# Hymba-style decoder step: norm weights moved into the output projection's rows, block-diagonals of the exponents written by ScalarE

## The chip, the cores and the metric

One core of one Trainium2 chip. The metric is the device time of one launch in microseconds (us). TensorE (PE; PEld is its weight load), VectorE (DVE), ScalarE (ACT), GpSimd (POOL) and SyncE (SP, which only issues transfers) run their own instruction streams in order and wait for each other through semaphores.

## The reference

One layer of a hybrid decoder runs on a prompt of 16 + 1024 tokens and on 8 running sequences of 4 tokens. Width 1024; two mixers of width 512 side by side; an MLP of width 4096. All is float32.

```python
def rmsnorm(x, g):
    return x * lax.rsqrt(jnp.mean(x * x, -1, keepdims=True) + EPS) * g

u = rmsnorm(h, norm1_g) @ w_in            # q, k, v, z, xbc, dt
ao = sliding_window_attention(q, k, v)    # window 128, with sinks
so = rmsnorm(ssd_scan(conv(xbc), dt) * silu(z), ssm_out_g)
mix = concatenate([rmsnorm(ao, attn_out_g), so], -1)      # 512 + 512
h = h + mix @ w_out                       # w_out: 1024 x 1024
u = relu(rmsnorm(h, norm2_g) @ w_up)
h = h + (u * u) @ w_down
y = rmsnorm(h, norm_f_g)
```

Since `(x * g) @ W = x @ (g[:, None] * W)`, the weights `attn_out_g` and `ssm_out_g` can stand on the mixers' outputs or on the rows of `w_out`.

## The kernel before, in words

Activations lie transposed: features on the 128 partitions, tokens in the free dimension. Tokens are cut in tiles of 128 (a small first tile of 48 holds the running sequences and the meta tokens) and, for the projections, in three chunks of 384, 384 and 288 columns. Every float32 operand of a large product is split in a rounded part and a remainder (hi and lo), and three products are added; `gemm` does this (all its matmuls carry line 202).

The stages in time:

- 0 to about 300 us: input projection, convolution and, per tile, `attn_block` and `norm_o`.
- about 300 to 407 us: the SSD per tile (`ssd`, `gate`), between pieces of the first half of the output projection (`wout_stream`: attention rows of `w_out`, eight row blocks m by three chunks). `exponents` prepares two groups of four tiles, near 306 and near 352 us: L, Tr and R, block-diagonal operands of small matmuls.
- about 407 to 457 us: the second half (`mixer_half`: SSD rows of `w_out`), chunks 0 and 1 first, then chunk 2, for which the eight blocks are loaded a second time. Of each m, GpSimd issues a transfer `he<-ha`; the squares for the next norm are summed, and GpSimd takes its power (`rs`, line 321).
- 457 us to the end: the MLP.

`load_wout` is called 24 times, 16 for `m` and `half` and 8 for the second pass of chunk 2. It transfers a raw block of 128x512 (SP's queue), ScalarE casts it (hi, line 243), and GpSimd or VectorE takes the remainder (lo, line 244). The raw tiles, `wraw`, come from a ring of two buffers, hi and lo from two rings of two. `Ahead` calls it one to three blocks ahead of use.

`norm_o` and `gate` end with four VectorE instructions (j = 0..3) that multiply a 128x128 quarter of the tile by its column of `vec` (the norm weight) and by the reciprocal root, which stands in PSUM.

Before the first SSD tile, GpSimd loads `selr` (line 909) and copies the small tile's columns to `xs0` and `bc0` (lines 944 and 946; the trace names them xs and bc). TensorE transposes them at lines 1038 and 1040.

The order of each engine's instructions is not the order of the Python code alone. The build sets it with a list scheduler, which follows operands, buffers and its own costs, so an edit also moves instructions that it does not touch.

Of the kernel before, what the change touches and what calls it, by code (L numbers as in the profile page):

```python
# [11 lines left out]
AF = mybir.ActivationFunctionType  # L12
ALU = mybir.AluOpType
# [37 lines left out]
def _consts():  # L51
    p = np.arange(128)[:, None]
    f = np.arange(128)[None, :]
    cols = {}
    parts = []
    at = [0]

    def put(name, a):
        a = np.asarray(a, np.float32)
        full = np.zeros((128, a.shape[1]), np.float32)  # L60
        full[:a.shape[0]] = a
        cols[name] = (at[0], at[0] + a.shape[1])
        at[0] += a.shape[1]
        parts.append(full)

    put("ident", np.eye(128))
    put("tri", (p <= f))
    blk = np.zeros((48, 48))
    for b in range(8):
        blk[4 * b:4 * b + 4, 4 * b:4 * b + 4] = 1  # L70
    blk[32:, 32:] = 1
    put("tri0", blk * (np.arange(48)[:, None] <= np.arange(48)[None, :]))
    put("blk0", blk)
    delta = np.zeros((128, 8))
    mm = np.zeros((128, 2))
    sel = np.zeros((128, 4, 128))
    for r in range(128):
        k = r % 32
        delta[r, k % 8] = 1
        if k < 16:  # L80
            for j in range(4):
                for hh in range(2):
                    if k % 8 == 2 * j + hh:
                        sel[r, j, hh * 64:hh * 64 + 64] = 1
            mm[r] = (0, 1)
        else:
            mm[r] = (1, 0)
    put("delta", delta)
    put("mm", mm)
    put("seqm", np.tile(np.kron(np.eye(8), np.ones((4, 1))), (3, 1)))  # L90
    resident = at[0]
    put("sel", sel.reshape(128, 512))


    pos = np.zeros(T, np.float32)
    for t in range(T):
        pos[t] = 4096 + t % 4 if t < NSAMP else t - NSAMP
    inv = (500000.0 ** (-np.arange(8) / 8.0)).astype(np.float32)
    ang = (pos[None, :] * inv[:, None]).astype(np.float32).astype(np.float64)
    cos, sin = np.ones((128, T)), np.zeros((128, T))  # L100
    for g in range(2):
        for half in range(2):
            rows = slice(64 * g + 8 * half, 64 * g + 8 * half + 8)
            cos[rows], sin[rows] = np.cos(ang), np.sin(ang) * (1 if half else -1)
    put("cos", cos)
    put("sin", sin)
    attn = at[0]

    prev, cur = np.where(f > p, 0.0, NEG), np.where(f <= p, 0.0, NEG)
    put("mask", np.concatenate([prev, cur, prev], axis=1))  # L110
    m1 = np.full((128, 48), NEG)
    for m in range(16):
        m1[:112 + m, 32 + m] = 0.0
    put("mask1", np.concatenate([m1, cur], axis=1))
    ms = np.full((2, 128, 160), NEG)
    for s in range(2):
        for r in range(128):
            b, t = 4 * s + r // 32, r % 4
            ms[s, r, t + 1:128] = 0.0
            ms[s, r, 128 + 4 * b:128 + 4 * b + t + 1] = 0.0  # L120
    put("maskS", ms.transpose(1, 0, 2).reshape(128, 320))

    cols["resident"], cols["rope_"], cols["attn_"] = (0, resident), (attn - 2 * T, attn), (attn, at[0])
    return np.concatenate(parts, axis=1), cols
# [62 lines left out]
def f(ap):  # L187
    return ap.bitcast(F32)
# [3 lines left out]
def body(ctx: ExitStack, tc: tile.TileContext, xT, xm, win, wdt, wo, wu, wd, ck, cv, sc, st, sT, vec, consts,  # L192
# [44 lines left out]
    def load_wout(m, half, eng=POOL):  # L237

        raw = raw_tile()[:, 0:4, :]
        SP.dma_start(out=raw, in_=wo[m, half])  # L240
        tag = "wlo" if m % 2 else "whi"
        hl = wring.tile([128, 2, 4, 128], F32R, name=tag, tag=tag, bufs=2)
        ACT.copy(out=hl[:, 0], in_=raw)
        eng.tensor_tensor(out=hl[:, 1], in0=raw, in1=f(hl[:, 0]), op=ALU.subtract)
        return hl[:, 0], hl[:, 1]
# [508 lines left out]
    def norm_o(i, o_ps=None):  # L754
# [2 lines left out]
        sq = pa.tile([128, 4, 128], F32, name="sqo", tag="sqo", bufs=1)  # L757
        ACT.activation(out=sq[:, :, :rows], in_=o if o_ps is None else o_ps[:, :, :rows], func=AF.Square)
        ps = yield from rms_bcast(pa, POOL, ps_tile, sq[:, :, :rows], rows, 512, "o", "pt")
        for j in range(4):  # L760
            DVE.scalar_tensor_tensor(out=o[:, j], in0=o[:, j], scalar=vec[:, V_GA + j:V_GA + j + 1], in1=ps[:, :rows],
                                     op0=ALU.mult, op1=ALU.mult)

    def attn_sample():
        kcT, vc = caches
# [147 lines left out]
    def exponents(rows, w, s):  # L913
        n = w // 32
        tp = ptile()
        PE.transpose(tp[:w, :rows], A4[:rows, s, :], ident[:rows, :rows])
        if n > 1:
            L = sp.tile([128, 4, 128], F32R, name="L", tag="L", bufs=1)
            Tr = sp.tile([128, 4, 128], F32R, name="Tr", tag="Tr", bufs=1)
            R = sp.tile([128, 8, 128], F32R, name="R", tag="R", bufs=1)  # L920
            POOL.memset(f(L), 0.0)
            POOL.memset(f(Tr), 0.0)
        else:
            L = sp.tile([128, 1, T0], F32R, name="L0")
            Tr = sp.tile([128, 1, T0], F32R, name="Tr0")
# [3 lines left out]
        for h in range(0, 8, 4):  # L929
            DVE.tensor_tensor(out=R[:w, h:h + 4, :rows], in0=tm[:w, :rows].unsqueeze(1).broadcast_to([w, 4, rows]),  # L930
                              in1=c("delta", w)[:, h:h + 4].unsqueeze(2).broadcast_to([w, 4, rows]), op=ALU.mult)
        for q in range(n):
            rr = slice(32 * q, 32 * q + 32)
            DVE.tensor_scalar(out=L[rr, q, :rows], in0=tp[rr, :rows], scalar1=mmc[rr, 0:1], scalar2=mmc[rr, 1:2],
                              op0=ALU.mult, op1=ALU.add)
# [233 lines left out]
    def gate(i):  # L1169
# [7 lines left out]
        ACT.activation(out=sq[:, :, :rows], in_=y, func=AF.Square)  # L1177
        yield
        ps = yield from rms_bcast(sp, DVE, ptile, sq[:, :, :rows], rows, 512)
        for j in range(4):  # L1180
            DVE.scalar_tensor_tensor(out=y[:, j], in0=y[:, j], scalar=vec[:, V_GS + j:V_GS + j + 1], in1=ps[:, :rows],
                                     op0=ALU.mult, op1=ALU.mult)
        hi, lo = act_cols(X, i)
        ACT.copy(out=hi, in_=y)
        POOL.tensor_tensor(out=lo, in0=y, in1=f(hi), op=ALU.subtract)
# [645 lines left out]
```

## Time and profile before

| | |
|---|---|
| median of 3 runs | 1131.54 us (1131.04 to 1132.6) |
| profiled execution | 1130.17 us, of which the span is 1128.4 us |
| busy, share of the span | TensorE 98%, VectorE 75%, ScalarE 50%, GpSimd 20% |
| granted TensorE clock | 0.998 |
| loads of `w_out` blocks | 24 of 256 KB, median 3.0 us from issue to landing |

The times shown are those of one launch; the profile is one execution of it, whose time is slightly below the median. In the profile, a group of instructions shares line, engine, operation and tile; the chain of waits is followed back from the last instruction to what released each step.

### The profile page before, as it was taken

How to read it: one execution, taken by the hardware profiler on the slowest of the kernel's cores; microseconds unless marked ns; L12 is line 12 of the kernel's file. 1: busy time of each engine (PE TensorE's matmuls, PEld its weight loads, DVE VectorE, ACT ScalarE, POOL GpSimd, SP SyncE). 2: the span in 40 equal slices, each digit the busy share in tenths (PEclk: the TensorE clock that was granted, in tenths of full speed). 3: DMA queues.
4: the chain of work that ended last, by engine and by line, in shares of the span. 5: the costliest groups of instructions: out<-in, count | busy, mean ns of one | idle time of the engine just before them, and what ended most of it. 6: DMA issues, size and time to landing. Idle time of an engine off the chain costs nothing.

```text
span 1128.4 us, 21816 instructions
## 1 busy us (share of the span) xinstructions
PE 1110.6 (98%) x8405; PEld 1071.9 (95%) x8405; DVE 841.9 (75%) x1649; ACT 567.6 (50%) x1200; POOL 225.0 (20%) x292
## 2 busy tenths in 40 slices
PE   9999999999999999999999999999999999999997
PEld 8989988989888899999999999999999999999996
DVE  6646888985698968998877777766599656768483
ACT  8312456575575748854444444444434334546461
POOL 0442365654444441210000000000000000000010
PEclk9999999999999999999999999999999999999999
DMA  8131101111476476666652443425999653465273
GB/s 289 68 98 38 38 23 35 39 49 46 136 217 194 147 260 227 212 186 220 211 189 106 162 152 134 176 92 176 374 310 322 197 173 103 125 196 166 77 228 107
DMA packets 84424, 177.64 MB, mean 157 GB/s; under 512 B 10692, under 2 KB 32740, under 8 KB 82272
## 3 DMA queue, kind: packets, MB, share of 16 engines
q1 hardware_dynamic: 77392, 141.58, 40.1%
q0 software_dynamic: 6224, 33.74, 7.5%
q8 instruction: 66, 1.08, 0.4%
q10 hardware_dynamic: 704, 0.93, 0.2%
q14 instruction: 38, 0.31, 0.1%
HBM read 125.49 MB, written 50.72 MB: 156 GB/s over the span
## 4 chain that ended last, share of the span: by engine, by line
PE 81%; DVE 7%; ACT 6%; issue 2%; DMA 2%; POOL 1%; SPq 0%; POOLq 0%; DVEq 0%; ACTq 0%
PE g L202 43%; PE b L202 21%; PE c L202 10%; PE s L202 3%; ACT p L677 1%; PE o L202 1%; DVE Qs L708 1%; DMA wraw<-in_win 1%; PE y L202 1%; PE pt L741 1%; DVE p L675 1%; ACT whi L231 1%; PE pt L202 0%; DVE xs L524 0%; ACT acth L407 0%
## 5 line engine op out<-in xcount | busy, mean ns | idle before, releaser
L202 PE MATMUL g<-acth,whi 128*128 128x384 f32 (+2 forms) x528 | 161.7, 330 | 0.2 <-DVE qT L454 0.2
L202 PE MATMUL g<-acth,wlo 128*128 128x384 f32 (+2 forms) x528 | 159.3, 327 | 0.2 <-DVE hb L985 0.2
L202 PE MATMUL g<-actl,whi 128*128 128x384 f32 (+2 forms) x432 | 140.7, 326 | 0.0
L1613 ACT CAST ts<-tr 128x528 fp32r<-128x528 f32 x92 | 58.2, 632 | 116.3 <-PE b L202 97.3
L1614 DVE TENSOR_TENSOR ts<-tr,ts 128x528 fp32r<-128x528 f32 x92 | 65.1, 707 | 54.9 <-ACT ts L1613 54.2
L202 PEld LDWEIGHTS g<-acth,whi 128*128 128x128 f32 x528 | 97.3, 188 | 2.0 <-issue 1.0
L202 PEld LDWEIGHTS g<-acth,wlo 128*128 128x128 f32 x528 | 97.1, 188 | 0.6 <-DVE hb L985 0.4
L202 PEld LDWEIGHTS g<-actl,whi 128*128 128x128 f32 x432 | 81.4, 188 | 0.2
L321 POOL TENSOR_TENSOR rs<-rs,nhalf 128x3 f32<-128x3 f32 x9 | 10.6, 1179 | 333.2 <-DMA wdq<-in_wd 284.9
L1329 ACT COPY s<-g 128x264 f32<-128x264 f32 x90 | 33.8, 376 | 61.7 <-PE g L202 61.1
L234 POOL TENSOR_TENSOR wlo<-wraw,whi 128x256 fp32r<-128x256 f32 x56 | 49.9, 921 | 11.4 <-ACT whi L231 11.3
L1402 POOL DMA_DIRECT2D u<-u x16 | 8.5, 532 | 176.3 <-ACT u L1345 146.9
L1334 DVE TENSOR_TENSOR u<-b,s 128x264 f32<-128x264 f32 x64 | 27.5, 430 | 19.2 <-PE b L202 9.8
L731 POOL TENSOR_TENSOR p<-p,sm 128x512 f32<-128x512 f32 (+1 forms) x32 | 34.9, 1112 | 30.2 <-DVE sm L729 28.4
L1339 ACT ACTIVATE u<-u 128x528 f32<-128x528 f32 x42 | 27.2, 647 | 26.6 <-DVE u L1338 26.6
L202 PE MATMUL b<-ts,w7y 128*128 128x264 f32 x279 | 39.3, 285 | 0.0
L202 PE MATMUL g<-ts,whi 128*128 128x264 f32 x279 | 38.9, 284 | 0.0
L202 PE MATMUL g<-ts,w7y 128*128 128x264 f32 x279 | 38.9, 283 | 0.0
L202 PE MATMUL b<-ts,whi 128*128 128x264 f32 x279 | 38.9, 284 | 0.0
L202 PE MATMUL g<-ts,wlo 128*128 128x264 f32 x270 | 38.0, 285 | 0.0
L202 PE MATMUL b<-ts,wlo 128*128 128x264 f32 x270 | 37.3, 282 | 0.0
L677 ACT ACTIVATE p<-p,nm 128x257 f32<-128x257 f32 (+1 forms) x64 | 31.3, 492 | 10.1 <-DVE nm L675 10.0
(580 smaller groups left out, 3479.1 us busy)
## 6 DMA issues: line engine op xcount, KB each, us to landing
tr<-u SPq DMA_DIRECT2D x92, 264.0 KB, 3.0
wraw<-in_wu SPq DMA_DIRECT2D x38, 512.0 KB, 4.1
wdr<-in_wd SPq DMA_DIRECT2D x68, 256.0 KB, 3.8
u<-t POOLq DMA_DIRECT2D x16, 1056.0 KB, 5.5
wraw<-in_win SPq DMA_DIRECT2D x16, 512.0 KB, 3.7
u<-u POOLq DMA_DIRECT2D x10, 792.0 KB, 3.6
wraw<-in_wo SPq DMA_DIRECT2D x24, 256.0 KB, 3.0
h<-he SPq DMA_DIRECT2D x16, 264.0 KB, 4.7
```

Of the source, the lines that this page charges most:

```text
L202: PE.matmul(out, lhsT=a, rhs=b, start=start, stop=stop, skip_group_check=on)
L231: ACT.copy(out=hi[:, k], in_=raw[:, k])
L234: eng.tensor_tensor(out=lo[:, n], in0=raw[:, n], in1=f(hi[:, n]), op=ALU.subtract)
L675: DVE.tensor_tensor_reduce(out=s_out[:, 0:W], in0=ps, in1=mask, scale=-scale, scalar=nsink, op0=ALU.add, op1=ALU.min, accum_out=nm)
L677: ACT.activation(out=s_out[:, 0:W + 1], in_=s_out[:, 0:W + 1], func=AF.Exp, bias=nm, scale=-1.0, accum_out=sm)
L708: DVE.tensor_tensor(out=Q[oth, g, :, :rows], in0=src, in1=f(Q[own, g, :, :rows]), op=ALU.subtract)
L731: POOL.tensor_tensor(out=p[:rows, r:r + 2, :W], in0=p[:rows, r:r + 2, :W], in1=sm[:rows, r:r + 2].unsqueeze(2).broadcast_to([rows, 2, W]), ...
L1329: ACT.copy(out=s[:, c], in_=ps[c][:, :TQ])
L1334: DVE.tensor_tensor(out=out[:, c], in0=ps[c][:, :TQ], in1=s[:, c], op=ALU.add)
L1339: ACT.activation(out=x, in_=x, func=AF.Square)
L1613: ACT.copy(out=t[:, 0], in_=x)
L1614: DVE.tensor_tensor(out=t[:, 1], in0=x, in1=f(t[:, 0]), op=ALU.subtract)
```

## The change

The norm weights no longer act on the mixers' outputs. `load_wout` multiplies each raw block's four row groups by the weights on GpSimd, in place, between the transfer and the cast (4 x 128 columns, the weight read with stride 0). The four instructions at the end of `norm_o` and of `gate` become one `tensor_tensor` of 128x512. In `exponents`, the groups of four write each of the four blocks of L and Tr whole, 128 partitions with zeros from a mask in the constants (`ownL`, `own`), by ScalarE; the memsets of GpSimd, the four VectorE instructions for L and the four narrow copies for Tr are gone. The small tile keeps its form.

```diff
+    own = np.arange(128)[:, None] // 32 == np.arange(4)[None, :]
+    put("ownL", np.concatenate([own * mm[:, 0:1], own * mm[:, 1:2]], axis=1))
+    put("own", own)
...
         raw = raw_tile()[:, 0:4, :]
         SP.dma_start(out=raw, in_=wo[m, half])
+        g = vec[:, V_GS:V_GS + 4] if half else vec[:, V_GA:V_GA + 4]
+        POOL.tensor_tensor(out=raw, in0=raw, in1=g.unsqueeze(2).broadcast_to([128, 4, 128]), op=ALU.mult)
...
-        for j in range(4):
-            DVE.scalar_tensor_tensor(out=o[:, j], in0=o[:, j], scalar=vec[:, V_GA + j:V_GA + j + 1], in1=ps[:, :rows],
-                                     op0=ALU.mult, op1=ALU.mult)
+        DVE.tensor_tensor(out=o, in0=o, in1=ps[:, :rows].unsqueeze(1).broadcast_to([128, 4, rows]), op=ALU.mult)
...
-            POOL.memset(f(L), 0.0)
-            POOL.memset(f(Tr), 0.0)
...
-        for q in range(n):
+        for q in range(n if n > 1 else 0):
+            sL, own = c("ownL"), c("own")
+            ACT.activation(out=L[:, q], in_=tp[:, :128], func=AF.Identity, scale=sL[:, q:q + 1], bias=sL[:, 4 + q:5 + q])
+            ACT.activation(out=Tr[:, q], in_=tp[:, :128], func=AF.Copy, scale=own[:, q:q + 1])
+        for q in range(n if n == 1 else 0):
...
-        for j in range(4):
-            DVE.scalar_tensor_tensor(out=y[:, j], in0=y[:, j], scalar=vec[:, V_GS + j:V_GS + j + 1], in1=ps[:, :rows],
-                                     op0=ALU.mult, op1=ALU.mult)
+        DVE.tensor_tensor(out=y, in0=y, in1=ps[:, :rows].unsqueeze(1).broadcast_to([128, 4, rows]), op=ALU.mult)
```

The lines shift by 4 to 6 (L244 becomes L250, L909 L913, L944 L950, L1480 L1484); the new product is L246, the transfer L243.

GpSimd at the start of the SSD, before: the last remainders of two early blocks (L244), a power of the norm (L321), then the load of `selr` and the copies.

```order
L244 TENSOR_TENSOR whi<-wraw,whi 128x512
L321 TENSOR_TENSOR rsb<-rsb,nhalf 128x1
L244 TENSOR_TENSOR wlo<-wraw,wlo 128x512
L909 DMA selr<-in_consts 128x512
L944 COPY xs_3280<-xs 128x4x32
L946 COPY xs_3280<-xs 128x4x16
L944 COPY bc_3281<-bc 128x4x32
L946 COPY bc_3281<-bc 128x4x16
L921 MEMSET L 128x512
L922 MEMSET Tr 128x512
```

GpSimd at the same place, after:

```order
L250 TENSOR_TENSOR whi<-wraw,whi 128x512
L327 TENSOR_TENSOR rsb<-rsb,nhalf 128x1
L250 TENSOR_TENSOR wlo<-wraw,wlo 128x512
L246 TENSOR_TENSOR wraw<-wraw,vec 128x512 x2
L913 DMA selr<-in_consts 128x512
L950 COPY xs_3254<-xs 128x4x32
L952 COPY xs_3254<-xs 128x4x16
L950 COPY bc_3255<-bc 128x4x32
L952 COPY bc_3255<-bc 128x4x16
```

The products of the next two blocks now stand ahead of `selr` and the copies; the memsets are gone.

GpSimd in the second half of the output projection (chunk 2), before: transfers `he` and the powers alone.

```order
L966 TENSOR_TENSOR sq_4722<-sq_4722,s_4851 128x384
L1480 DMA he<-ha 128x384
L321 TENSOR_TENSOR rs_5132<-rs_5132,nhalf 128x3
L1480 DMA he<-ha 128x384 x3
L321 TENSOR_TENSOR rs_5225<-rs_5225,nhalf 128x3
L1480 DMA he<-ha 128x384 x4
```

After:

```order
L972 TENSOR_TENSOR sq_4677<-sq_4677,s_4807 128x384
L246 TENSOR_TENSOR wraw<-wraw,vec 128x512 x6
L1484 DMA he<-ha 128x384
L327 TENSOR_TENSOR rs_5094<-rs_5094,nhalf 128x3
L246 TENSOR_TENSOR wraw<-wraw,vec 128x512
L1484 DMA he<-ha 128x384
L246 TENSOR_TENSOR wraw<-wraw,vec 128x512
L1484 DMA he<-ha 128x384
L327 TENSOR_TENSOR rs_5190<-rs_5190,nhalf 128x3
L246 TENSOR_TENSOR wraw<-wraw,vec 128x512 x2
L1484 DMA he<-ha 128x384 x2
L246 TENSOR_TENSOR wraw<-wraw,vec 128x512
```

The eleven last products (the last three blocks of chunks 0 and 1, and m = 0 to 7 of chunk 2) now share the queue with them: m = 3 comes behind the first `he` and the first power, m = 5 and 6 behind the second power, m = 7 behind two more transfers.

SP's queue at the end of that stage, before:

```order
L240 DMA wraw<-in_wo 128x512 x2
L1290 DMA wraw_5231<-in_wu 128x1024
L1290 DMA wraw_5233<-in_wu 128x1024
L240 DMA wraw<-in_wo 128x512 x2
L1290 DMA wraw_5272<-in_wu 128x1024
```

After:

```order
L243 DMA wraw<-in_wo 128x512 x2
L1294 DMA wraw_5196<-in_wu 128x1024
L1294 DMA wraw_5198<-in_wu 128x1024
L243 DMA wraw<-in_wo 128x512 x3
L1294 DMA wraw_5238<-in_wu 128x1024
```

Three instead of two loads of `w_out` blocks now follow the first two loads of the MLP's weights (`wu`).

VectorE at the second group of exponents, before:

```order
L930 TENSOR_TENSOR R<-tm,cs 128x512 x2
L934 TENSOR_SCALAR L<-s,cs 32x128
L985 TENSOR_TENSOR hb<-hb,g 128x384
L934 TENSOR_SCALAR L<-s,cs 32x128
L1181 SCALAR_TENSOR_TENSOR xs<-xs,vec,s 128x128 x2
L934 TENSOR_SCALAR L<-s,cs 32x128
L1181 SCALAR_TENSOR_TENSOR xs<-xs,vec,s 128x128 x2
L934 TENSOR_SCALAR L<-s,cs 32x128
L1088 TENSOR_TENSOR hn<-hn,s 128x512
```

After:

```order
L932 TENSOR_TENSOR R<-tm,cs 128x512 x2
L991 TENSOR_TENSOR hb<-hb,g 128x384
L1186 TENSOR_TENSOR xs<-xs,s 128x4x128
L1104 TENSOR_TENSOR xs<-xs,y 128x4x128
L1094 TENSOR_TENSOR hn<-hn,s 128x512
```

The four writes of L are gone from VectorE's stream, and the gate's product is one instruction.

## The prediction

> **What bounds the kernel now.** I read the page first (busy shares, then the chain of waits), then busy times by stretch, then the chain, the engines' timelines and the groups of lines at the places the change touches.
>
> ```profile
> PE 1110.6 (98%) x8405; PEld 1071.9 (95%) x8405; DVE 841.9 (75%) x1649; ACT 567.6 (50%) x1200; POOL 225.0 (20%) x292
> PE 81%; DVE 7%; ACT 6%; issue 2%; DMA 2%; POOL 1%; SPq 0%; POOLq 0%; DVEq 0%; ACTq 0%
> ```
>
> TensorE is busy in 98% of the span, yet only 81% of the chain is TensorE; 13% is VectorE and ScalarE. The stretches (columns: PE, PEld, DVE, ACT and POOL busy, granted clock, DMA share, GB/s) say where those can be:
>
> ```profile
> 200.00:250.00 50.00, 49.39 (x315) 44.37 (x314) 46.03 (x99) 31.15 (x81) 29.70 (x35) 1.00 0.14 42
> 300.00:350.00 50.00, 49.44 (x382) 42.26 (x382) 43.97 (x91) 34.96 (x93) 24.97 (x27) 1.00 0.73 223
> 400.00:450.00 50.00, 50.00 (x324) 49.65 (x323) 36.08 (x79) 31.33 (x57) 15.15 (x17) 1.00 0.77 262
> sum 400.00, PE 393.37 PEld 363.18 DVE 328.56 ACT 250.55 POOL 172.29; mean PE 49.17 PEld 45.40 DVE 41.07 ACT 31.32 POOL 21.54
> ```
>
> The last row sums 100 to 500 us: TensorE is idle for 400.00 − 393.37 = 6.6 us there. That is about all that a faster VectorE or ScalarE can win. A new wait that stops TensorE is added in full, because from 400 us on it has no idle time to absorb it. The clock stays at 1.00, so it plays no part.
>
> **The chain where the change works**, in order of time (start, us, what):
>
> ```profile
> 188.71 1.13 DVE qT L761 x4
> 300.63 1.12 DVE qT L761 x4
> 312.19 1.17 ACT Mt L1063 x2
> 353.82 0.40 DVE L L934
> 354.26 0.60 DVE xs L1181 x2
> 354.89 0.41 DVE L L934
> 355.33 0.32 DVE xs L1181
> 355.97 0.42 DVE L L934
> ```
>
> Among eight attention tiles the four norm products (L761) are on the chain twice. In the second SSD group the block-diagonal `L` (L934) and the gate's products (L1181) lie on it one after the other; in the first group, around 312 us, it is ScalarE that ends last.
>
> Prices (groups: busy us, mean ns; the ACT row is from the timeline: start, us):
>
> ```profile
> L761 DVE SCALAR_TENSOR_TENSOR qT<-qT,vec,pt 128x128 f32<-128x128 f32 x32 | 9.2, 343 | 1.4 <-PE pt L202 1.4
> L1097 DVE TENSOR_TENSOR eA<-f,eA 128x512 f32<-128x512 f32 x8 | 5.5, 684 | 0.3
> L1044 ACT ACTIVATE xs<-xs,vec 128x128 f32<-128x128 f32 x32 | 10.5, 400 | 0.1
> L1051 POOL TENSOR_TENSOR xw<-xd,te 128x512 f32<-128x512 f32 x8 | 9.2, 1150 | 14.1 <-DVE xd L1049 14.0
> L1100 DVE TENSOR_TENSOR xs<-xs,eA 128x512 f32<-128x512 f32 x8 | 8.3, 1042 | 0.1
> 353.42 0.26 ACT L936 CAST Tr<-s 32x128 fp32r<-32x128 f32 x1 [2.75 <-DVE L L934]
> ```
>
> **1. Norm products, one operation a tile.** Four instructions take 1.12 us (row at 300.63). One 128x512 product with a PSUM operand takes 0.68 (L1097). So 0.44 us less a tile, 8 × 0.44 = 3.5 us of VectorE in attention and as much in the gate. In attention two of eight are on the chain: −0.9, rounded to −1.0 for what follows them; ends 0 (others end last anyway) and −2.5 (the part of the 6.6 us idle that lies there, at most).
>
> **2. Exponents.** Per group of four tiles VectorE loses 4 × 0.40 = 1.6 us (L934), GpSimd its two memsets. ScalarE gets 8 × 0.40 (L1044: same shape, also a scaled copy) for 4 × 0.26, so +2.2 us. In the second group VectorE is on the chain: the three quoted pieces of L give −1.2, the fourth and the gate's products about −0.6. In the first group ScalarE ends last, so a part of its +2.2 comes back, about +0.8; the later gate tiles give −0.5. Sum −1.5; ends +1.5 (all eight operations delay the chain of the first group) and −3.5.
>
> **3. The weight product on GpSimd.** 24 of them, 128x512 with a stride-0 operand. Nearest row: L1051, 1.15 us with such an operand; ends 1.0 and 1.27 (the L244 row below). Taken: 1.1 us, 26 us in all on an engine with 172 of 400 us used. Most hide: in attention the products wait in gaps, and each output-projection weight is loaded early. Two places do not hide.
>
> *The start of the SSD.* POOL, SP's queue, the transfer's median (KB, us to landing), and TensorE:
>
> ```profile
> 299.58 1.27 POOL L244 TENSOR_TENSOR wlo<-wraw,wlo 128x512 fp32r<-128x512 f32 x1
> 300.80 0.77 POOL L909 DMA_DIRECT2D selr<-in_consts  x1
> 301.57 0.32 POOL L944 COPY xs<-xs 128x128 f32<-128x128 f32 x1
> 302.36 0.62 POOL L944 COPY bc<-bc 128x128 f32<-128x128 f32 x1
> 302.93 0.56 POOL L946 COPY bc<-bc 128x64 f32<-128x64 f32 x1
> 299.13 2.08 SPq L240 DMA_DIRECT2D wraw<-in_wo  x2
> wraw<-in_wo SPq DMA_DIRECT2D x2, 256.0 KB, 2.9
> 304.29 0.60 PE L1038 MATMUL s<-cs,xs 128*48 128x128 f32 x4
> 304.73 0.38 PE L1040 MATMUL s<-cs,bc 128*48 128x128 f32 x2
> ```
>
> Before, the copies to `xs0` and `bc0` follow the sub at once and end at 303.5, 0.8 us ahead of TensorE, which takes xs0 at 304.29. In the new order two weight products stand ahead of them, of the two loads that SP issues from 299.13 to 301.21. The second lands near 301.2 + 2.9 = 304.1, is multiplied until 305.2; then the selr issue (0.77, to 306.0), xs0 (302.36 − 301.57 = 0.8, to 306.8), bc0 (1.1, to 307.9). TensorE waits 306.8 − 304.3 = 2.5 for xs0; its four transposes take 0.44, then it waits 0.6 for bc0. Sum +3.1. TensorE's order ahead of these transposes is the same in both kernels, so nothing moves in between. Ends: +1.5 (the second load lands 1.6 us earlier, or other engines make up half) and +3.7.
>
> *The second half of the output projection.* Here raw weights go through a ring of two buffers: a load starts when the sub of the load before the last is through. DVE, SP, POOL, ACT, TensorE, and one piece of the chain (445.15):
>
> ```profile
> 439.68 0.69 DVE L244 TENSOR_TENSOR wlo<-wraw,wlo 128x512 fp32r<-128x512 f32 x1
> 438.96 1.77 SPq L240 DMA_DIRECT2D wraw<-in_wo  x2
> 440.07 0.63 POOL L1480 DMA_DIRECT2D he<-ha  x1 [18.72 <-DVE ha L960]
> 441.00 0.89 POOL L321 TENSOR_TENSOR rs<-rs,nhalf 128x3 f32<-128x3 f32 x1 [0.30 <-DVE rs L320]
> 445.15 4.11 DMA wraw<-in_wo
> 449.34 0.62 ACT L243 CAST whi<-wraw 128x512 fp32r<-128x512 f32 x1 [0.69 <-DMA wraw<-in_wo]
> 443.77 0.34 PE L202 MATMUL g<-acth,wlo 128*128 128x384 f32 x1
> 449.19 0.42 PE L202 MATMUL g<-acth,wlo 128*128 128x384 f32 x1
> 453.44 0.34 PE L202 MATMUL g<-acth,wlo 128*128 128x384 f32 x1
> ```
>
> The last load but one is on the chain: sub, transfer of 4.11, cast, at 449.34. Every load now has 1.1 us more, and GpSimd takes the products in a queue with `he` transfers and the powers of the norm.
> - m=3 (used at 443.77): its product stands behind the he transfer of m=0 and the power, so it starts at 441.89, ends at 443.0; cast (0.62) to 443.6, sub (0.69) to 444.3. TensorE uses hi first, lo one matmul or two later: wait 0.2.
> - m=5 (449.19) is issued when that sub frees the buffer: 444.3 instead of within 438.96 + 1.77 = 440.7. Landing 2.9 to 4.1 later, 447.2 to 448.4; product, cast, sub (2.4) to 449.6 or 450.8; the second power is ahead of it on POOL. TensorE needs lo at 449.5: wait 0.1 to 1.3, and I take 1.2 for the power.
> - m=7 (453.44, by then 454.9): issued at 450.8, landed 453.7 to 454.9, sub done 456.1 to 457.3; needed 455.3: wait 0.8 to 2.0, taken 1.3.
> Sum with 0.1 for the loads ahead: +2.8. Ends: +0.5 (all transfers short, powers not in the way) and +4.5; not below nothing, since no load gets shorter. SP also issues the last three of these loads behind both first MLP loads, which keeps me from the lower end. All that follows is TensorE's, so the shift reaches the end.
>
> The longer constants row (370 to 382 columns) is loaded long before its use: nothing.
>
> **Sum.** −1.0 − 1.5 + 3.1 + 2.8 = +3.4 us. The profiled execution took 1130.17 (span 1128.4), so 1133.6 by it; it stands 1.4 below the median 1131.54, and against that I say 1134.9. A change below 0.2% (2.3 us) cannot be told from none.
>
> **Rivals.**
> - *Only one GpSimd wait shows* (same). If the second load at 299 lands about 2 us earlier, or the ring keeps up, one term of about 3 falls away against −2.5: 1131.54 + 3.0 − 2.5 = 1132.0. For it: the ring's waits rest on landings of 2.9 to 4.1 us. Against: the order on POOL, which is fixed. 0.25.
> - *VectorE's relief decides* (faster). VectorE is busy 46.03 of 50 us at 200 and 43.97 at 300; if what it hands back frees TensorE in most of the 6.6 us idle, the gain is −2.5 − 3.5 = −6.0, and with about half of the two waits (2.9) the time is 1131.54 − 3.1 = 1128.4. It decides when the waits together are below 3.7 us. Against: only two of eight norm tiles are on the chain, and the first group's chain is ScalarE's, which gets more work. 0.18.
> - *VectorE is slowed by GpSimd's reads* (slower). L1100, with both operands in SBUF, has a mean of 1042 ns; L1097, same shape, one operand in PSUM, 684. So 0.36 us is lost per such instruction with GpSimd 25 of 50 us busy. 24 more products give 24 × 0.36 = 8.6 us of VectorE; with half of it on the path before 400 us (13 products, 2.3) and a third after (11 products, 1.3) this adds 3.6: 1138.5. For it: casts' subs (L244) have both operands in SBUF and are on the ring's path. Against: VectorE is 72% busy at 400 to 450. 0.15.
> The Trainium skill ("SBUF — State Buffer", section "Who interferes with whom") states that a VectorE instruction with two SBUF inputs and a GpSimd instruction that reads SBUF exclude one another for a whole instruction. By that rule L1100 against L1097 agrees with the trace, and the 24 products could hold VectorE for up to 24 × 1.1 = 26 us as an estimate, which would make the sum about 1160 if all were on the path; the measured 0.36 a piece says far less.
>
> **Numbers.** The forecast itself 0.42, same 0.25, faster 0.18, port 0.15: faster 0.18, same 0.25, slower 0.57. The range from 1128.2 to 1140.0 reaches just beyond the relief that decides and the port's case, and leaves out the full relief without waits (1125.5) and both upper ends together; the forecast's own is 1133.8 to 1137.5.
>
> **What would show it.** Right: a gap on TensorE of some 2.5 us before the transposes of xs0, with GpSimd in a weight product until just before the selr issue; gaps at m=5 and m=7 of chunk 2 with the cast waiting for GpSimd; the MLP of equal length, started 3 to 4 us later. Single norm products of about 0.68 us, weight products of about 1.1. Wrong: the second raw tile landed before 302, or the ring's loads issued as early as before; or a stretch from 100 to 300 us that is more than 2.5 us shorter; or L1100 and L244 clearly longer than now.

## Result and the profile after

The changed kernel takes 1145.89 us (median of 4 runs, 1143.15 to 1146.48) against 1131.43 us (4 runs, 1131.04 to 1132.6): ratio 1.0113, 95% interval 1.01 to 1.0127. The forecast had the right sign and a quarter of the size: +14.5 us instead of +3.4, and 5.9 us above the upper end of the range. Ratios here and below are estimates over executions in the same state, which leave out one of e3 at 3823.27 us, so they differ a little from the quotient of the medians (1.0128 here).

The profiled execution took 1145.79 us (span 1144.0). Its mean granted clock is 0.993, and it is 0.993 or 0.994 in all four; the 82 executions of before beside the experiments have 0.995 to 0.999, and 70 of them 0.997 or more.

The page after, busy time and the shares of the chain of waits:

```profile
PE 1119.8 (98%) x8405; PEld 1080.5 (94%) x8405; DVE 839.0 (73%) x1587; ACT 570.7 (50%) x1208; POOL 248.8 (22%) x312
PE 85%; DVE 6%; ACT 3%; DMA 2%; POOL 2%; issue 1%; POOLq 0%; DVEq 0%; SPq 0%; ACTq 0%
```

TensorE does the same 8405 matmuls in 9.2 us more busy time. Busy time that grows with no work added is the first sign that the clock has a part. The stretches (columns as before: PE, PEld, DVE, ACT, POOL busy, granted clock, DMA share, GB/s):

```profile
300.00:350.00 50.00, 46.98 (x338) 40.34 (x339) 37.97 (x74) 32.39 (x89) 24.19 (x24) 0.93 0.70 206
350.00:400.00 50.00, 46.87 (x347) 41.24 (x346) 41.28 (x78) 31.98 (x83) 25.89 (x24) 0.97 0.53 159
400.00:450.00 50.00, 47.77 (x310) 45.74 (x309) 34.69 (x65) 27.57 (x51) 21.13 (x22) 1.00 0.64 216
450.00:500.00 50.00, 48.38 (x344) 47.52 (x344) 44.75 (x64) 37.14 (x68) 18.27 (x25) 0.97 0.62 204
sum 400.00, PE 386.55 PEld 356.13 DVE 311.94 ACT 245.01 POOL 194.69; mean PE 48.32 PEld 44.52 DVE 38.99 ACT 30.63 POOL 24.34
```

Two things are new. TensorE is idle 400.00 − 386.55 = 13.45 us between 100 and 500, instead of 6.6. And the clock column falls below 1.00 in three rows (0.93 and twice 0.97). VectorE's 311.94 us instead of 328.56 are not its relief: the window holds less of the program (2595 matmuls instead of 2712). Over the whole span VectorE is busy 839.0 us instead of 841.9; without the products (e1 below) it is 829.5. So the edits relieve VectorE by some 12 us, and the products take 9.5 of them back. On the chain its share fell by 1 point and ScalarE's by 3, and TensorE's rose by 4: the end waits less often for the engines that were relieved, and it still comes later.

From here on a *shift* is the start of a TensorE instruction in a trace less the start of the same instruction in the trace of before. It says where time is lost. At the instructions that stood at 300, 325, 350, 405 and 458 us before, and at the last ones:

| kernel | 300 | 325 | 350 | 405 | 458 | end |
|---|---|---|---|---|---|---|
| after | 0.0 | 4.7 | 9.7 | 8.0 | 14.3 | 15.9 |

So 4.7 us go at the start of the SSD, 5.0 in its second group of tiles, 1.7 come back in the rest of it, 6.3 go in the second half of the output projection, and 1.6 in the MLP. TensorE's waits from 300 to 460 us (longest groups: total, times, longest):

```profile
PE s L205 <- ACT Mt L1069: 2.6, 1, 2.6
PE s L1044 <- POOL xs L952: 2.4, 1, 2.4
PE c L205 <- DVE sq L972: 1.7, 1, 1.7
```

The second is the wait that was forecast; the other two were not. They are taken in order of time.

**The start of the SSD.** GpSimd and TensorE (start, us, what; in brackets the idle time before and its end):

```profile
301.84 1.04 POOL L246 TENSOR_TENSOR wraw<-wraw,vec 128x512 f32<-128x512 f32 x1 [0.99 <-DMA wraw<-in_wo]
304.58 1.04 POOL L246 TENSOR_TENSOR wraw<-wraw,vec 128x512 f32<-128x512 f32 x1 [1.70 <-DMA wraw<-in_wo]
305.56 0.77 POOL L913 DMA_DIRECT2D selr<-in_consts  x1
306.34 0.30 POOL L950 COPY xs<-xs 128x128 f32<-128x128 f32 x1
...
306.87 0.62 PE L1044 MATMUL s<-cs,xs 128*48 128x128 f32 x4 [2.42 <-POOL xs L952]
...
311.57 0.52 PE L205 MATMUL g<-actl,wlo 128*128 128x384 f32 x1
```

GpSimd stands with an empty engine at 302.9 because the head of its queue wants a transfer, and everything behind it waits too. The products end at 305.6 (forecast 305.2), TensorE starts at 306.87 (forecast 306.8). But the last row is odd: a 384-column product of 0.52 us, where the rows of before have 0.34 to 0.42. Stretches of 2 us show why:

```profile
308.00:310.00 2.00, 2.00 (x7) 1.14 (x7) 2.00 (x6) 1.74 (x6) 1.03 (x1) 0.50 0.60 192
310.00:312.00 2.00, 2.00 (x8) 1.95 (x9) 1.95 (x5) 2.00 (x7) 0.00 (x0) 0.50 0.89 182
...
314.00:316.00 2.00, 2.00 (x16) 1.96 (x14) 0.41 (x1) 0.73 (x3) 0.00 (x0) 0.81 0.94 253
356.00:358.00 2.00, 2.00 (x7) 2.00 (x7) 2.00 (x7) 0.69 (x3) 0.00 (x0) 0.50 0.87 248
452.00:454.00 2.00, 2.00 (x8) 2.00 (x7) 1.73 (x2) 0.70 (x2) 1.25 (x2) 0.50 0.84 291
```

Behind each of the three waits, 1.1 to 1.7 us after its end, the granted clock falls to 0.50: for 6.8 us after the first, for 3.4 us after each of the others. TensorE counts as busy for all of that and does less (0.52 us for the product of 384 columns). At half clock the three stretches cost (6.83 + 3.41 + 3.41) / 2 = 6.83 us, if TensorE would not have waited for others in them. With the 6.82 us of added idle time that makes 13.65 us; the shift grows by 14.2 us from 100 to 500 us.

**The second SSD group.** The chain of waits at that place (start, us, what):

```profile
344.99 5.95 DMA wraw<-in_wo
...
351.08 1.04 POOL wraw L246
352.12 0.96 POOL rsb L327
...
353.11 0.40 ACT dg L382
353.51 0.49 ACT Mt L1069
...
354.04 0.66 PE s L205 x4
```

A transfer of a weight block took 5.95 us, twice the median of 3.0. The product stood at the head of GpSimd's queue for it, the power of a norm stood behind the product, ScalarE's diagonal waited for the power, ScalarE's `Mt` stood behind that, and TensorE waited for `Mt`. None of these has anything to do with the weight.

**The second half of the output projection.** VectorE, GpSimd and TensorE:

```profile
444.92 0.45 DVE L972 TENSOR_TENSOR sq<-sq,s 128x288 f32<-128x288 f32 x1
446.83 0.55 DVE L972 TENSOR_TENSOR sq<-sq,s 128x384 f32<-128x384 f32 x1
448.13 1.21 POOL L246 TENSOR_TENSOR wraw<-wraw,vec 128x512 f32<-128x512 f32 x1 [3.67 <-DMA wraw<-in_wo]
448.36 1.29 DVE L972 TENSOR_TENSOR sq<-sq,s 128x288 f32<-128x288 f32 x1
449.80 0.80 PE L205 MATMUL c<-ones,sq 128*128 128x1 f32 x6 [1.66 <-DVE sq L972]
...
462.43 1.33 DVE L250 TENSOR_TENSOR wlo<-wraw,wlo 128x512 fp32r<-128x512 f32 x1
...
462.45 0.44 PE L205 MATMUL g<-acth,wlo 128*128 128x384 f32 x1 [0.61 <-ACT wlo L249]
463.82 0.62 PE L205 MATMUL g<-acth,wlo 128*128 128x384 f32 x2 [0.75 <-DVE wlo L250]
```

The square L972 of 288 columns takes 1.29 us beside the product; one of the same form took 0.45 at 444.92. It ends 0.3 us after the product does. At m=5 the forecast wait for the cast is there (0.61), and the sub behind it takes 1.33 us instead of 0.69, again beside GpSimd's products; TensorE waits 0.75 us for that sub.

The prices of the products came out as forecast, those of the norm products in the gate (0.68 in the median) as in attention (instruction views: durations min/median/max in ns, first and last start):

```profile
L246 POOL TENSOR_TENSOR wraw<-wraw,vec x24: 1030/1042/1499, 253.9 to 466.6; 128x512 f32<-128x512 f32 x24
L766 DVE TENSOR_TENSOR qT<-qT,pt x9: 273/677/686, 131.6 to 300.6; 128x512 f32<-128x512 f32 x8, 128x128 f32<-128x128 f32 x1
```

### The profile page after: what moved, and what is told of

The parts are those of the page before. It is cut to its first block, busy times and chain, and to the rows that moved or that the text cites. A ratio compares the mean times of both kernels' runs of the same rounds, so it can differ in the third digit from the quotient of the medians.

```text
span 1144.0 us, 21778 instructions
## 1 busy us (share of the span) xinstructions
PE 1119.8 (98%) x8405; PEld 1080.5 (94%) x8405; DVE 839.0 (73%) x1587; ACT 570.7 (50%) x1208; POOL 248.8 (22%) x312
## 4 chain that ended last, share of the span: by engine, by line
PE 85%; DVE 6%; ACT 3%; DMA 2%; POOL 2%; issue 1%; POOLq 0%; DVEq 0%; SPq 0%; ACTq 0%
PE g L205 44%; PE b L205 21%; PE c L205 10%; PE s L205 4%; PE o L205 2%; DMA wraw<-in_wo 1%; DMA wraw<-in_win 1%; PE pt L205 1%; PE pt L747 1%; PE y L205 1%; PE f L205 1%; POOL wraw L246 1%; DVE Qs L714 1%; ACT p L683 1%; POOL p L737 0%
## 5 line engine op out<-in xcount | busy, mean ns | idle before, releaser
L205 PE MATMUL g<-acth,wlo 128*128 128x384 f32 (+2 forms) x528 | 163.5, 335 | 1.8 <-DVE wlo L250 0.9
L205 PEld LDWEIGHTS g<-acth,wlo 128*128 128x128 f32 x528 | 99.4, 193 | 3.5 <-DVE wlo L250 1.7
L205 PEld LDWEIGHTS g<-ts,w7y 128*128 128x128 f32 x279 | 36.4, 188 | 0.0
```

The source lines that it names most:

```text
L205: PE.matmul(out, lhsT=a, rhs=b, start=start, stop=stop, skip_group_check=on)
```

## Experiments

Medians, ratios and shifts of all experiments, for reference below. Before has a shift of 0 throughout; each shift is from one profiled execution, and 2.0 of the 2.2 us that e2 has at 300 are there at 50 us, ahead of every product. Each ratio is to executions of before taken beside the run, whose median is 1132.27 us for e1 to e4, 1133.15 for e5 to e8, 1132.45 for e9 to e12 and 1131.89 for e13 and e14; so the ratios can be compared, and the medians only within such a group:

| kernel | median, us | ratio (95%) | 300 | 325 | 350 | 405 | 458 | end |
|---|---|---|---|---|---|---|---|---|
| after | 1145.89 | 1.0113 (1.01–1.0127) | 0.0 | 4.7 | 9.7 | 8.0 | 14.3 | 15.9 |
| e1_no_mul | 1131.41 | 0.9994 (0.9985–1.0003) | 0.3 | 2.0 | 2.1 | 0.3 | −0.3 | 2.6 |
| e2_mul_only | 1149.1 | 1.0149 (1.0135–1.0163) | 2.2 | 7.2 | 10.9 | 10.8 | 18.5 | 19.2 |
| e3_exp_only | 1133.25 | 1.001 (1.0–1.002) | 1.2 | 0.8 | 1.0 | −1.5 | 0.2 | 2.5 |
| e4_mul_dve | 1142.06 | 1.0094 (1.008–1.0109) | −0.4 | 1.8 | 1.9 | 1.6 | 8.1 | 12.3 |
| e5_touch | 1139.57 | 1.0054 (1.0037–1.0071) | 0.3 | 4.6 | 7.5 | 5.9 | 6.9 | 9.5 |
| e6_work_only | 1140.09 | 1.0057 (1.0042–1.0072) | 1.6 | 1.2 | 3.3 | 2.5 | 6.3 | 9.0 |
| e7_half0 | 1136.93 | 1.0033 (1.0023–1.0043) | 0.4 | 6.5 | 7.3 | 5.5 | 4.9 | 8.5 |
| e8_order | 1148.51 | 1.0132 (1.0116–1.0148) | 0.6 | 4.6 | 5.4 | 3.8 | 16.1 | 17.5 |
| e9_pad12 | 1134.34 | 1.0021 (1.0012–1.003) | 0.9 | 2.5 | 2.3 | 2.3 | 2.4 | 4.0 |
| e10_exp_pad | 1131.6 | 0.9993 (0.9984–1.0001) | 0.9 | 0.5 | 0.7 | −1.9 | −0.2 | 0.75 |
| e11_fill_half0 | 1135.61 | 1.0029 (1.0019–1.004) | −0.7 | 2.6 | 3.7 | 1.9 | 1.8 | 5.9 |
| e12_exp2_pad | 1131.8 | 0.9998 (0.9989–1.0007) | 1.5 | 1.6 | 1.7 | −1.2 | 0.4 | 2.4 |
| e13_work_write | 1132.77 | 1.0004 (0.9991–1.0017) | 0.0 | 0.5 | 1.1 | −0.6 | −1.1 | 2.2 |
| e14_exp_pad32 | 1130.67 | 0.9986 (0.9976–0.9996) | 0.0 | 0.0 | −0.1 | −2.7 | −1.1 | 0.8 |

### Which edit costs the time

**e1_no_mul**: after, without the weight product.

```diff
-        POOL.tensor_tensor(out=raw, in0=raw, in1=g.unsqueeze(2).broadcast_to([128, 4, 128]), op=ALU.mult)
```

> The changed kernel without the weight product in the loads (the norm weights are left out). Waits theory (the 24 products hold up GpSimd's queue at three places, TensorE stands, and its clock is halved after each): none of the three gaps, clock 1.00 throughout, 1130 us (1128.5 to 1131.5). Rival, the other edits and the new order they bring cost part of it: 1134 or more.

**e2_mul_only**: before, with the product added and nothing else.

```diff
+        g = vec[:, V_GS:V_GS + 4] if half else vec[:, V_GA:V_GA + 4]
+        POOL.tensor_tensor(out=raw, in0=raw, in1=g.unsqueeze(2).broadcast_to([128, 4, 128]), op=ALU.mult)
```

> The kernel before plus only the weight product on GpSimd (the weights act twice). Waits theory: nearly the whole loss, 1143 to 1148 us, with gaps of 2 us and more on TensorE and granted clock 0.5 behind them. Rival, part of the loss is from the norm products and exponents: 1138 or less.

**e3_exp_only**: before, with the exponents' edit and its constants and nothing else.

```diff
+    put("ownL", np.concatenate([own * mm[:, 0:1], own * mm[:, 1:2]], axis=1))
+    put("own", own)
...
-            POOL.memset(f(L), 0.0)
-            POOL.memset(f(Tr), 0.0)
...
+            ACT.activation(out=L[:, q], in_=tp[:, :128], func=AF.Identity, scale=sL[:, q:q + 1], bias=sL[:, 4 + q:5 + q])
+            ACT.activation(out=Tr[:, q], in_=tp[:, :128], func=AF.Copy, scale=own[:, q:q + 1])
```

> The kernel before plus only the exponents edit. Waits theory: 1131.4 less 0 to 1.5 us (VectorE's relief in the second group against ScalarE's load in the first), no gap over 1.2 us on TensorE. Rival, ScalarE's eight wide writes in a row hold up the chain: 1133 or more.

Measured: the whole change without the products is even with before (0.9994); the products alone cost 1.49%, more than the whole change. So the products are the entire loss, and they can be placed by taking e1's shifts from after's: 2.7 us by 325, 4.9 from 325 to 350, 0.1 by 405, 6.9 by 458, together 14.6. Full clock throughout was expected of e1, and its trace does not have it: 3.4 us are at half clock from 308.7. e3 and e1 also give the relief: with the same constants, e1 (which has the norm products) is at 300 us 0.9 us ahead of e3 (which has not), where −1.0 was forecast. That fits and does not show it, since e3 and e14, which have the same attention, differ by 1.2 us there. e3 gains 2.5 us between 350 and 405, behind the second group of exponents. Yet e3 as a whole gains nothing (1.001): 1.7 us go between 405 and 458 and 2.3 in the MLP. That the MLP gets longer has nothing to do with exponents, and is taken up below.

### Is it the wait or the work

**e5_touch**: after, with a product of 4 columns instead of 512. GpSimd still waits for each transfer and the cast for GpSimd, but there is next to no work (the other weights are left out).

```diff
-        POOL.tensor_tensor(out=raw, in0=raw, in1=g.unsqueeze(2).broadcast_to([128, 4, 128]), op=ALU.mult)
+        POOL.tensor_tensor(out=raw[:, 0, 0:4], in0=raw[:, 0, 0:4], in1=g, op=ALU.mult)
```

> The changed kernel with the product cut to 4 columns of the raw tile (128x4, about 0.1 us): GpSimd waits for each transfer as before, in the same order of its queue, but has next to no work (norm weights left out). Waits theory (GpSimd stands at the head of its queue until a transfer has landed): half or more of the loss stays, ratio to the kernel before 1.005 to 1.010, the gaps at xs0 and in the second SSD group are there, about 1 us shorter each. Rival, the 26 us of work or its reads make the loss: ratio 0.998 to 1.002.

**e6_work_only**: the same work on other data, into a buffer that is overwritten later; GpSimd waits for no transfer (weights left out).

```diff
-        POOL.tensor_tensor(out=raw, in0=raw, in1=g.unsqueeze(2).broadcast_to([128, 4, 128]), op=ALU.mult)
+        POOL.tensor_tensor(out=hl[:, 1], in0=ident.unsqueeze(1).broadcast_to([128, 4, 128]), in1=g.unsqueeze(2).broadcast_to([128, 4, 128]), op=ALU.mult)
```

> The changed kernel with the 24 products reading constants instead of the raw tile and writing to the lo tile ahead of its remainder (norm weights left out): the work stays on GpSimd, the wait for the transfer is gone. Waits theory: ratio 0.998 to 1.004, no gap over 1.2 us on TensorE in the SSD stage. Rival, work or reads: ratio 1.009 to 1.013.

**e13_work_write**: e6, with the product replaced by two memsets of the same buffer: as long on GpSimd, but it reads nothing.

```diff
+        for _ in range(2):
+            POOL.memset(f(hl[:, 1]), 0.0)
```

> As the kernel with the work alone, but each product replaced by two memsets of the lo tile on GpSimd (0.52 us each), which write and read nothing (norm weights left out). Contention theory (a VectorE instruction with two SBUF operands stands while GpSimd reads): no VectorE remainder, square sum or dg over 0.75 us from 440 to 460, shift from 405 to 458 us at most +1.5 (work alone: +3.8). Rival, GpSimd's time in its queue makes it: +3 to +4 again.

The wait alone costs 0.54%, the work alone 0.57% (between what the theory and its rival had expected), and the work that reads nothing costs nothing (1.0004, interval over 1). Each mostly belongs to a place of its own. In the SSD it is the wait: e5 has shifted 5.9 us by 405, e6 2.5, of which 1.6 were there at 300. e6 was expected to have no stop over 1.2 us in the SSD and has one of 1.7 us at 328.6 (for a VectorE copy), after one of 2.2 us at 299.5; so the work is not free ahead of 405 either. e5's trace has the same two stops; TensorE's waits from 300 to 460, and GpSimd at the second:

```profile
PE s L205 <- ACT Mt L1069: 2.8, 1, 2.8
PE s L1044 <- POOL xs L952: 1.9, 1, 1.9
```

```profile
351.68 0.20 POOL L246 TENSOR_TENSOR wraw<-wraw,vec 128x4 f32<-128x4 f32 x1 [4.81 <-DMA wraw<-in_wo]
351.83 0.55 POOL L327 TENSOR_TENSOR rsb<-rsb,nhalf 128x1 f32<-128x1 f32 x1
```

The product takes 0.20 us and the power 0.55; what TensorE waits 2.8 us for is that GpSimd's queue stood 4.81 us for a transfer.

In the second half it is the work: e6 loses 3.8 us between 405 and 458, e5 1.0. e6's GpSimd and VectorE there:

```profile
449.65 1.05 POOL L248 TENSOR_TENSOR whi<-cs,vec 128x512 fp32r<-128x512 f32 x1
...
453.10 1.05 POOL L248 TENSOR_TENSOR wlo<-cs,vec 128x512 fp32r<-128x512 f32 x1
449.24 2.02 DVE L250 TENSOR_TENSOR whi<-wraw,whi 128x512 fp32r<-128x512 f32 x1
...
452.74 2.54 DVE L1231 TENSOR_TENSOR xb21l<-ha,xb21h 128x1056 fp32r<-128x1056 f32 x1
```

and e13's, whose memsets take 1.11 us for two:

```profile
443.71 1.11 POOL L249 MEMSET whi<- 128x512 f32 x2 [0.23 <-ACT b L977]
...
445.81 1.11 POOL L249 MEMSET wlo<- 128x512 f32 x2 [0.25 <-PE g L205]
445.27 1.25 DVE L1232 TENSOR_TENSOR xb21l<-ha,xb21h 128x1056 fp32r<-128x1056 f32 x1
446.44 0.68 DVE L251 TENSOR_TENSOR wlo<-wraw,wlo 128x512 fp32r<-128x512 f32 x1
```

A sub of 512 columns takes 0.68 us while GpSimd's memset runs (445.81 to 446.92) and 2.02 beside its product; the same 1056-column sub 1.25 and 2.54. Beside these products a VectorE instruction with both operands in SBUF took 1.3 us longer, somewhat more than the product itself (1.05). Of e6's lost 3.8 us, TensorE's waits make 2.9: 0.9 and 1.6 us for the casts' subs and 0.4 us for a square; the other 0.9 us are not traced. The Trainium skill ("SBUF — State Buffer", section "Who interferes with whom") states this rule, with the exception for a GpSimd instruction that only writes; e6 against e13 agrees in both halves.

The two effects do not add up simply in the second half: 1.0 + 3.8 is 4.8, and after lost 6.3. The difference is about the size of the stretch at half clock there, 1.7 us, which e6 and e5 do not have in that part; that it is this stretch is not shown.

**e4_mul_dve**: after, with the products on VectorE.

```diff
-        POOL.tensor_tensor(out=raw, in0=raw, in1=g.unsqueeze(2).broadcast_to([128, 4, 128]), op=ALU.mult)
+        DVE.tensor_tensor(out=raw, in0=raw, in1=g.unsqueeze(2).broadcast_to([128, 4, 128]), op=ALU.mult)
```

> The changed kernel with the 24 weight products on VectorE instead of GpSimd. Waits theory: the copies to xs0 and the powers no longer stand behind a product, but VectorE's queue does where a load lands late; 1134 to 1142 us, the gap at xs0 gone. Rival, shared reads of GpSimd and VectorE made the loss: 1130 to 1133, since GpSimd reads nothing more than before.

Measured 1.0094. The loss in the SSD is all but gone (1.6 us at 405), that of the second half is not (6.5 us). There the product stands at the head of VectorE's queue instead. The longest wait of TensorE from 300 to 475 us, and VectorE before it:

```profile
PE g L205 <- ACT whi L249: 2.3, 1, 2.3
```

```profile
451.29 0.69 DVE L246 TENSOR_TENSOR wraw<-wraw,vec 128x512 f32<-128x512 f32 x1 [1.08 <-DMA wraw<-in_wo]
```

A faster engine (0.69 instead of 1.04 us) does not help when an engine that works in order is made to wait for a transfer.

### The two places apart, and the order

**e7_half0**: after, with the products of the first half alone (the gate's weights left out).

```diff
-        POOL.tensor_tensor(out=raw, in0=raw, in1=g.unsqueeze(2).broadcast_to([128, 4, 128]), op=ALU.mult)
+        if not half:
+            POOL.tensor_tensor(out=raw, in0=raw, in1=g.unsqueeze(2).broadcast_to([128, 4, 128]), op=ALU.mult)
```

> The changed kernel with the products for the attention half alone (8 of 24, the SSD's norm weights left out). Waits theory: only the stall at the start of the SSD stays, with the half clock behind it: +2.5 to +5 us at 330 us, partly won back, ratio 1.002 to 1.006; no gap in the second SSD group or in the second half. Rival, an equal price for each product: a third of the loss, 1.004, but spread over all places.

Measured 1.0033. It has the wait at 304 and not that of the second group, whose transfer belongs to the second half. From 300 to 405 it loses 5.1 us where e1 loses nothing. Its wait for xs0 is 2.40 us; the clock is then at half for 10.2 us in this execution, the slowest of its ten.

**e11_fill_half0**: e7, with nine matmuls put into the gap, whose results nobody uses.

```diff
+        for _ in range(9 if i == 0 else 0):
+            mm(px[:, 0:128], ones, f(X[2][1][0][:, 3, 160:288]), True, True)
```

> The kernel with products for the attention half alone, plus nine matmuls of 128x128 without use on TensorE just ahead of the transposes of xs0, where it stands for 2.4 us. The wait itself stays. Clock theory (standing is followed by some microseconds at half clock): granted clock 1.00 from 300 to 340, shift against the kernel before at 330 us +3 to +4.5 instead of +6.5 to +7, ratio 1.000 to 1.003. Rival, the half clock costs nothing since TensorE waits for others there: shift at 330 us unchanged or longer, ratio 1.003 to 1.005.

One stretch of e7, and the same of e11:

```profile
310.00:312.00 2.00, 2.00 (x8) 1.51 (x8) 2.00 (x5) 2.00 (x8) 0.18 (x1) 0.50 0.79 170
```

```profile
310.00:312.00 2.00, 2.00 (x13) 1.75 (x11) 1.91 (x5) 2.00 (x9) 0.00 (x0) 1.00 0.48 151
```

The transposes of `xs0` are as late as in e7 (the shift grows by 3.5 us from 300 to 305, there by 3.3), and yet the shift at 405 is 1.9 instead of 5.5 us. TensorE still stands for 1.27 us ahead of the added matmuls, and the clock stays at 1.00. The other executions agree: e7's mean clock is 0.994 to 0.996 in all ten, where before had 0.996 to 0.998 beside it; e11's is 0.998 or 0.999 in seven of eight, where before had 0.995 to 0.999. The totals do not show the 3.6 us (ratios 1.0029 and 1.0033, intervals overlapping): in e11's profile 2.8 us go between 458 and 500 instead of e7's 1.8, with a wait of 1.25 us for ScalarE at 502 in its own time. That the half clock costs time at its place is shown by this pair of traces; that a filler is worth putting in is not.

**e8_order**: after, with a tiny chain of GpSimd operations that holds some products back until the copies at the start of the SSD, or the last power, are through.

```diff
+        if "bc0" in behind and ((not half and m > 3) or (half and m < 5)):
+            g = late(g, behind["rs" if half else "bc0"])
```

> The changed kernel, all 24 products on GpSimd, but some get their weights through a tiny copy that depends on the copies to bc0 (m 4 to 7 of the attention half) or on the latest power (m 0 to 4 of the SSD half), so they stand behind these in GpSimd's queue instead of ahead. Waits theory: the gaps at xs0 and in the second SSD group vanish, that of the second half stays: ratio 1.004 to 1.008, and the shift against the kernel before at 405 us is within 2 us. Rival, work or reads: ratio 1.010 to 1.014, shift at 405 us 6 us or more.

This was meant as the repair, and it missed: 1.0132. That is the rival's ratio, but not its shift of 6 us or more at 405. Both stops in the SSD are gone, and three others stand in their place (TensorE's waits, 300 to 475):

```profile
PE g L205 <- ACT whi L260: 3.5, 1, 3.5
PE s L1058 <- ACT Tr L950: 2.7, 1, 2.7
PE g L205 <- DVE whi L261: 2.4, 1, 2.4
```

The held products now stand ahead of the next GpSimd work of the SSD (2.7), and loads come late in the second half (3.5 and 2.4; 12.3 us of shift from 405 to 458). The shift at 405 is 3.8 instead of 8.0. Read this way, moving a waiting instruction within a full queue changed who stands behind it; no run isolates the new stops.

### The constants row

e3 and e1 lose 2 to 3 us in the MLP, which the edits do not touch. All they share there is a constants row 12 columns longer, which puts every tile allocated after it 48 bytes further on.

**e9_pad12**: before, with 12 unused columns.

```diff
+    put("pad", np.zeros((128, 12)))
```

> The kernel before plus 12 columns of zeros in the resident constants and nothing else, so every later tile lies 48 bytes further in SBUF. In the traces so far all kernels with the longer constants lose time evenly through the MLP (0.36 us from 500 to 600, 2.3 to 2.9 us from 458 to the end), the one with the product alone does not. Placement theory: the same even loss here, 1 us from 500 to 850, ratio 1.001 to 1.003. Rival, the loss comes with the other edits or with the run: no drift, ratio 0.999 to 1.001.

**e10_exp_pad**: e3, with 4 more columns (64 bytes in all).

```diff
+    put("pad", np.zeros((128, 4)))
```

> The exponents edit alone with its 12 new constant columns filled up to 16, so that later tiles move by 64 bytes instead of 48. Placement theory: no drift in the MLP, the gain at the second SSD group shows: ratio 0.998 to 0.9995. Rival, no effect of placement: like the exponents edit alone, 1.001, with the drift.

**e14_exp_pad32**: e3, with 20 more columns (128 bytes in all).

```diff
+    put("pad", np.zeros((128, 20)))
```

> The exponents edit alone, constants filled up by 32 columns: later tiles move by 128 bytes. Placement theory, steps of 128 bytes: no drift in the MLP (with 64 bytes 0.18 us per 100 us stayed, with 48 0.36), ratio 0.997 to 0.999. Rival, any longer constants cost: drift of 0.18 or more per 100 us, ratio 0.999 to 1.001.

**e12_exp2_pad**: e10, with the first group's exponents left as they were.

```diff
-        for q in range(n if n > 1 else 0):
+        for q in range(n if s.start > 1 else 0):
```

> The exponents edit for the second group of four tiles alone, constants filled up to 16 columns. Theory: ScalarE's eight writes hold up the first group, where its queue is the last to end, and help in the second, where VectorE's was: 1 us less than with both groups, ratio 0.997 to 0.9985. Rival, the first group costs nothing: the same as with both.

Twelve unused columns cost 0.21% (0.12 to 0.3), 2.4 us. In e9's one trace, whose end has shifted by 4.0 us, 1.6 us lie in the MLP; ahead of it stands a stretch of 3.4 us at half clock from 309.0, which the other executions need not have (eight of eleven have a mean clock of 0.998 or 0.999, this one 0.997). The stretch from 500 to 600 us, MLP only, of before, of e9 and of e14:

```profile
500.00:600.00 100.00, 100.00 (x826) 100.00 (x825) 80.68 (x142) 46.36 (x94) 6.38 (x12) 1.00 0.55 183
```

```profile
500.00:600.00 100.00, 100.00 (x821) 99.81 (x821) 80.64 (x141) 46.07 (x95) 6.79 (x13) 1.00 0.56 189
```

```profile
500.00:600.00 100.00, 100.00 (x825) 100.00 (x825) 80.39 (x141) 45.63 (x92) 6.92 (x13) 1.00 0.53 181
```

Same matmuls, TensorE busy throughout, clock 1.00, and 821 instead of 826 go through in 100 us. The shifts say it more finely: from 500 to 850 us they grow by 1.2 us in e9 and by 1.0 in every other kernel with 48 bytes more, by 0.55 with 64 bytes (e10, e12), by 0.5 with 128 (e14) and by 0.0 in e2, which has no new constants. So none of the longer rows is free, against what was expected of e10 and e14. After 850 us another 0.2 to 1.4 us go, 1.4 in e3 and in e14 alike; that part does not follow the bytes, and its cause is open. What about the placement matters is not settled either: no run moved one tile alone.

e14 is the fastest kernel of all, 1130.67 us, ratio 0.9986 (0.9976 to 0.9996): the exponents' edit is worth 0.14% where the placement costs less, 2.7 us at 405 in its trace. e12 against e10 was to show whether the eight ScalarE operations in the first group cost anything; the two totals are even (0.9998 and 0.9993, intervals overlapping).

## Why the prediction was wrong

- **"The clock stays at 1.00, so it plays no part."** The first step that failed, and the largest: a term put at nothing that is about 6.8 us in the trace after. Of these, 1.7 us lie in a stretch that e1 has at the same place without any product. The 1.00 was read from one execution of a kernel whose longest stop of TensorE was 1.2 us, and carried over to one with three stops of 1.7 to 2.6 us. e11 shows the mechanism at one place: the stop at 304 was filled in part, and the clock stayed. Nor is before always at full clock: of its 82 executions, the 12 with a mean clock of 0.995 or 0.996 took 1134.4 us in the median, the 53 with 0.998 or 0.999 1131.7.
- **"Most hide."** The forecast looked for products on a path of their own and found two places. The third, the second SSD group, was passed over because the weight there is loaded early and the product does hide; the *queue* behind it does not. The wait of 2.6 us and 1.7 us of half clock make 4.3 of the 4.9 us lost there. e5, which has next to no work, has the wait (2.8 us), without the half clock. The forecast had named this effect at the start of the SSD, and did not ask the same of the other products ahead of a power.
- **The start of the SSD, forecast +3.1.** Right in mechanism, place and size as far as the wait goes: 2.42 us for xs0 against 2.5; the 0.6 for bc0 was not there (GpSimd's copies took 0.54 and 0.52 us instead of the 0.8 and 1.1 assumed).
- **The second half, forecast +2.8, measured 6.9 against e1.** The waits for a late cast and its sub are there: 1.36 us at m=5 (0.61 and 0.75) and 0.26 at m=7, against the 1.2 and 1.3 of the forecast. Most of the rest is the rival with a chance of 0.15, VectorE held by GpSimd's reads: e6 loses 3.8 us there without any wait for a transfer. The rival's sum for VectorE, 8.6 us, was about right (after is busy 839.0 us, e1 829.5); what it had wrong is how much of it stands on the path, 1.3 us behind 400. It spread 0.36 us over every instruction; one that does meet a product loses 0.6 to 1.3 us at once (1.33 for 0.68, 1.29 for 0.45, in e6 2.02 for 0.68 and 2.54 for 1.25), and TensorE waits, since it has no idle time there. "VectorE is 72% busy" was no argument against it: the share doesn't say whether its instruction of that moment is the one awaited.
- **"The longer constants row: nothing."** Another term put at nothing: +2.4 us by e9, of which the steady loss in the MLP from 500 to 850 us is 1.0 to 1.2. No row of before could show it.
- **Norm products, −1.0.** Right in the price, 0.68 us each. The −0.9 us between e1 and e3 fits, but single traces do not measure so little.
- **Exponents and gate, −1.5.** In the SSD the gain is larger (−2.7 us from 300 to 405 in e3). ScalarE's eight writes in the first group took 2.5 us (309.89 to 312.36 in after) instead of the 3.2 assumed. About 1.7 of the gain is lost by 458 (in e14 1.6, with 1.0 us of waits for a late cast and its sub), and the rest in the MLP.
- **The rivals.** "VectorE's relief decides" priced the relief at −6.0 us; the most that any run shows is −2.7 us at 405 and 0.14% in total (e14), and all edits without the products give 0.9994. "Only one wait shows" failed outright: more waits showed, not fewer.

What stays open: why half clock follows some stops and not others (below), what in the placement slows the MLP, what else costs time after 850 us, and 0.5 us of the excess from 100 to 500 that neither idle time nor clock explains.

## What to carry to other kernels

An operation put between a transfer and its use puts a wait for that transfer at the head of an in-order queue: list everything behind it on that queue, at every place and not only where its own result is urgent, and use long landings (here 5.95 us) rather than the median. Where TensorE is the bound, count a possible stretch at half clock behind each new stop of 1.7 us or more: here the three together cost as much again as the stops. Before work moves to GpSimd, look on VectorE for instructions with two SBUF operands on the path beside it, and give an unrelated constant's size a run of its own.

## What the hardware showed

- **Half clock after short stops.** It followed stops of 2.42, 2.57 and 1.66 us after, for 6.8, 3.4 and 3.4 us; in e7 2.40 us, for 10.2; in e5 1.85 us, for 6.8. The Trainium skill ("TensorE: Matmul & The Clock Gate", section "What's actually happening") puts the clock down to half after an idle window of about 3.4 us. The lengths of the stretches here agree with such a window; the stops do not, each being shorter than it. Nor does the length of a stop decide: e2 stood 2.72 us at 353.85, e5 2.8 us at its second SSD group and e6 2.17 us at 299.5, and all kept full clock behind it, while e1 and e9 had 3.4 us at half clock from 308.7 and 309.0 with no stop above 0.93 us in the 100 us ahead of it. In that stretch the matmuls are small and follow one another loosely, which may count as well; no run tells.
- **VectorE against GpSimd.** A VectorE instruction with both operands in SBUF stood for a GpSimd product that reads SBUF and takes 1.05 us (2.02 us instead of 0.68), and not at all for a memset, which only writes (0.68).
- **48 bytes.** Moving the tiles by 48 bytes let 821 instead of 826 matmuls through in 100 us (e9), at clock 1.00 and with TensorE busy throughout; 64 and 128 bytes cost about half as much from 500 to 850 us.
